# Hybrid layer with expert retrieval: the first group's four tiles by fetched rows, the second group's four dense, routing weights built all at once

## The chip, the cores and the metric

The kernel runs on one core of one Trainium2 chip. The metric is the device time of one execution in microseconds (us), as the median of several runs. The engines are TensorE (PE in the profile, its weight loads PEld), VectorE (DVE), ScalarE (ACT), GpSimd (POOL) and SyncE (SP). SyncE and GpSimd issue the DMAs of this kernel; the 16 DMA engines of the core carry them all.

## The reference: what is computed

One layer of a hybrid backbone over a prompt (128 tokens) and a sample (1024 tokens), model width 1024. A combined projection feeds a gMLP mixer (A) and a bidirectional gated recurrence, HGRN2 (B); both are merged, projected and added to the residual. Then comes the part that the change is about, the retrieval over 16384 single-neuron experts:

```
h  = rmsnorm(x) * (1 + scale2) + shift2
q  = (h @ w_q)  as 8 heads x 2 halves x 128
s  = q . sub_keys                       # 8 x 2 x 128 scores a token
v1, i1 = top16(s[:, :, 0]);  v2, i2 = top16(s[:, :, 1])
top 16 of the 256 sums v1 + v2  ->  idx = i1 * 128 + i2,  g = softmax(top 16)
a  = gelu(h . u_tab[idx]) * g           # 128 experts a token
x  = x + gate2 * sum(a * v_tab[idx])
```

At the end every token gets a last rmsnorm. Only the prompt's recurrent states and the normalised tokens are returned.

## The kernel before

**Tiles.** Tokens stand in nine tiles of 128: tile 0 is the prompt, tiles 1 to 8 the sample. Products of the sample are computed in two float32r parts a factor, as three matmuls (helper `mmx`, L126 to L131: high x high, low x high, high x low); `split` (L98 to L100) makes the parts, the high one on ScalarE, the low one on VectorE.

**Stages, in order.** The modulation vectors and the whole prompt (to about 340 us, without its retrieval); HGRN over the sample (340 to 705); the first group GA = [5, 6, 7, 8] (705 to 1116) and the second group GB = [1, 2, 3, 4] (1116 to 1700), both in `group`: gate and value projections (12 units of weights), merge (24 units), output projection (8), norm and transposes, queries with scores and top 16 (16 units). Then the dense pass, and the last norms.

**Two ways of retrieval.** For the tiles in `GATHER` = [0, 1, 2, 3] the experts are fetched row by row (`gather`): for each of 128 chosen experts, one indirect DMA on GpSimd brings a row of `u_tab` for each of 128 tokens (128 x 4 KB), one VectorE instruction multiplies it by the tokens and sums; then, per head, 16 rows of `v_tab` are fetched and added with their weights. That is 256 row instructions a tile. For the tiles in `DENSE` = [5, 6, 7, 8, 4] all 16384 experts are computed: for each of 128 expert tiles e, `hidden` multiplies the tokens (640 columns in two halves of 320) by `u`, gelu follows, the result is multiplied by the routing weights `Gt` and split, and multiplied by `v`. The sums of RES = 3 token tiles stay in PSUM (`out_res`), those of ROT = 2 more rotate: every GI = 4 expert tiles they are added to SBUF by VectorE (`out_rot`).

**Choosing and building.** `combine` picks the 16 best sums of each head of one token tile, on VectorE; it is a generator with about a dozen steps, and can be run for heads 0 to 3 and 4 to 7 separately. For a dense tile, `build_G` then writes the routing weights as a matrix experts x tokens: for every OT = 4 tokens one step compares an iota with the two indices (L516), weights one of the one-hots by the high and low half of g (L520 on ScalarE or L524 on VectorE, every second step, and L526), TensorE multiplies the pairs (L543), ScalarE evacuates (L546), and blocks of 32 tokens go to DRAM (`G_d`).

**Order.** Instructions are ordered by a scheduler at build time, with program order as priority. Filling work comes from three queues of generators (`choose_q`, `build_q`, `gather_q`). In the groups every unit of weights (`unit`, `tick`) advances them by `rate`; in the dense pass `fill` advances the fetched rows at each of its main VectorE instructions, and `paced` keeps a row's instruction behind an earlier instruction of the main stream. GA's choices and builds run beside GB; tile 4 is chosen and built behind GB (L988 to L990), beside two early expert tiles. Tiles 1 to 3 lie in DRAM (`tvi_d`) and are chosen inside the dense pass (`combine_late`). The tokens of the dense tiles pass through DRAM (`h2T_d`) into `h2D`. Fetched rows have NGR = 4 slots, and NGD = 2 more in the dense pass.

Of the kernel before, what the change touches and what calls it, by code (L numbers as in the profile page):

```python
# [28 lines left out]
RATE2 = (3, 4.5, 2)  # L29
RQ = 0.3  # L30
LATE = (3, 0.8)
LEAD = 60
AH = (1, 2)       # of how many blocks of one-hots ScalarE does the weighting
RATE = (4, 2.6, 0.5, 2.5, 6.1, 4.5)
# [17 lines left out]
def hybrid_kernel(ctx, tc, x_all, pos, c2t, w_ada, b_ada, wst, wspt, bsp, lbraw, vecs, fng, skt, state,  # L52
# [19 lines left out]
    h2T_d = dram.tile([2, 128, 8, TD], F32, name="h2T_d")  # L72
    o_d = dram.tile([NT, 128, 512], F32, name="o_d")
    tvi_d = dram.tile([NT, 128, 512], F32, name="tvi_d")
    h2r_d = dram.tile([NT, 128, D], F32, name="h2r_d")

# [5 lines left out]
    vec = consts.tile([128, 24], F32, name="vec")        # g1(8) g2(8) sgu(4) hgrn(4), channel on partition  # L82
# [6 lines left out]
    lb = consts.tile([128, 3, 8], F32, name="lb")        # lb, (1-lb)/2, (1+lb)/2  # L89

# [33 lines left out]
    def mmx(ps, a, b, first, last):  # L124
        """a.T @ b for operands in one float32 part or in two float32r parts"""
# [24 lines left out]
    # work that fills the engines beside the main stream: generators, advanced a step at a time  # L150
# [42 lines left out]
    # order of the six modulation vectors: shift1 scale1 gate1 shift2 scale2 gate2  # L193
# [74 lines left out]
    def proj_rows(u0, opd, n, evac, native, half=None):  # L268
        """token-major product with a 512 wide block (4 units); opd(k): parts [128, T]; evac(i, psum)"""
# [16 lines left out]
    def hgrn(pool, blocks, proj, vsrc, states):  # L286
        """blocks: (token tile, head) of each 128 columns; proj(j, evac): products for q, fw, bw"""
        NB = len(blocks)
        NTOK = NB * 128
        K2 = pool.tile([128, 2, NTOK], F32, name="K2")       # fw, bw  # L290
        Q2 = pool.tile([128, 2, NTOK], F32, name="Q2")       # bw, fw
        F2 = pool.tile([128, 2, NTOK], F32, name="F2")       # fw, bw
# [41 lines left out]
            # K: fw first halves by the total of the second, bw second halves by the total of the first  # L334
# [8 lines left out]
            # totals of the doubled segments: the second level in T2, the others in place of the gates  # L343
# [7 lines left out]
        T128 = tbase                                        # F2[:, d, T128 + block]  # L351
# [52 lines left out]
    C = {}  # L404
    GA, GB = [5, 6, 7, 8], [1, 2, 3, 4]
# [9 lines left out]
    def combine(gp, t, tv, ti, al=None, c4=None, V=V, h0=0, h1=8, res=None):  # L415
        """the 16 best sums of a head: products of the two lists, with (i+1)(j+1) <= 16"""
# [28 lines left out]
        if res is None:  # L445
            res = al("res", 384).rearrange("p (a b) -> p a b", a=3)    # i1, i2, g
# [3 lines left out]
        hk = lambda x: x[:, :, None, :].to_broadcast(SH)                     # over the list position  # L450
        lp = lambda x: x[:, :, :, None].to_broadcast(SH)                     # over the chosen
# [26 lines left out]
        # softmax over the 16 of a head  # L478
# [10 lines left out]
        if t in GATHER:  # L489
            ga = gat.tile([128, 128], F32, name=f"ga{t}")  # L490
            V.tensor_copy(ga, res[:, 2])
            ix = gat.tile([128, 128], I32, name=f"ix{t}")
            V.scalar_tensor_tensor(ix, res[:, 0], 128.0, res[:, 1], op0=OP.mult, op1=OP.add)
            gather_q.append(gather(t, ga, ix))
        else:
# [3 lines left out]
            rt = gp.tile([128, 2, 128], F16, name="rt", bufs=4)      # i2, i1  # L499
            V.tensor_copy(rt, pt[:, 0:256].rearrange("p (a b) -> p a b", a=2))  # L500
            rg = gp.tile([128, 128], F32, name="rg", bufs=4)         # g (scaled)
# [6 lines left out]
    def build_G(gp, i, rt, rg, gl, tags):  # L508
        SH = [128, 2, 128, OT]

        def one_hots(t0):
# [675 lines left out]
```

## Time and profile before

| | |
|---|---|
| time, median of 3 runs | 3696.43 us (3687.48 to 3701.36) |
| profiled execution, span | 3697.6 us |
| PE busy | 3351.2 us (91%) |
| DVE busy | 2840.2 us (77%) |
| ACT busy | 1157.4 us (31%) |
| POOL busy | 1440.8 us (39%) |
| DMA | 971.12 MB, mean 263 GB/s |
| fetched rows | 512 + 512 indirect DMAs of 512 KB |

The profile is one execution. Its span runs from the first to the last instruction; it lies 1.2 us above the median of the runs, and no time around it is added. A stretch (a row of the view by windows) gives the busy time of each engine with its number of instructions, then the clock that TensorE was granted as a share of the full one, the share of the DMA engines' time, and GB/s. A matmul's duration contains its pipeline, so TensorE's pace is read from the distance of starts.

### The profile page before, as it was taken

To read this page: it belongs to the slowest core of one execution; us is meant where nothing else is said; L and a number is where in the kernel's file an instruction comes from. 1 tells how busy PE (TensorE), PEld (TensorE's weight loads), DVE (VectorE), ACT (ScalarE), POOL (GpSimd) and SP (SyncE) were. 2 spreads that over 40 slices of the span, in tenths; PEclk is the share of its full clock that TensorE was granted. 3 is DMA by queue.
4 is the path that set the end of the run, shared out by engine and by line. 5 is a ranking of instruction groups with operands and counts; after the bars stand their busy time and mean duration, and the time that the engine had idled before them with its cause. 6 is when DMAs were issued, how large, how long until landed. Compare 5 with 4: busy or idle time off the path is not lost. (4 is left out here: it accounts for less than half of the span.)

```text
span 3697.6 us, 48818 instructions
## 1 busy us (share of the span) xinstructions
PE 3351.2 (91%) x17547; PEld 2757.2 (75%) x17547; DVE 2840.2 (77%) x5427; ACT 1157.4 (31%) x2075; POOL 1440.8 (39%) x1128
## 2 busy tenths in 40 slices
PE   7787889899797899888789999889999989999997
PEld 3265678777476676576688989788888878898996
DVE  1315698787499987588787889888888888888888
ACT  2511233432222387735322222222222222222222
POOL 0100632265311220000255554556555465655664
PEclk9899999999898999888799999999999999999998
DMA  7676854488842476441798898889988799989986
GB/s 267 226 272 208 297 189 153 158 292 307 296 161 97 163 278 252 172 165 75 257 327 307 316 335 286 311 298 330 326 308 316 256 327 338 318 301 328 328 313 249
DMA packets 361957, 971.12 MB, mean 263 GB/s; under 512 B 32721, under 2 KB 142673, under 8 KB 356081
## 3 DMA queue, kind: packets, MB, share of 16 engines
q0 software_dynamic: 149824, 546.37, 41.6%
q1 hardware_dynamic: 211888, 421.62, 33.1%
q8 instruction: 138, 2.26, 0.2%
q14 instruction: 107, 0.87, 0.1%
HBM read 897.07 MB, written 70.80 MB: 262 GB/s over the span
## 5 line engine op out<-in xcount | busy, mean ns | idle before, releaser
L795 POOL DMA_INDIRECT gu<-in_urow_dram,ix x512 | 693.5, 1354 | 1024.8 <-DVE jk L798 368.8
L808 POOL DMA_INDIRECT gv<-in_vrow_dram,ix x512 | 694.7, 1357 | 720.6 <-DVE acc L813 388.2
L798 DVE SCALAR_TENSOR_TENSOR jk<-gu,h2r 128x1024 f16<-128x1024 f32 x512 | 624.9, 1220 | 125.0 <-DMA gu<-in_urow_dram,ix 118.7
L813 DVE SCALAR_TENSOR_TENSOR acc<-gv,act,acc 128x1024 f32<-128x1024 f32 x508 | 651.3, 1282 | 65.9 <-DMA gv<-in_vrow_dram,ix 57.9
L129 PE MATMUL pH<-h2DH,uH 128*128 128x320 f32 x2016 | 626.1, 311 | 11.3 <-DVE accd L1045 10.4
L131 PE MATMUL pH<-h2DH,uL 128*128 128x320 f32 x2016 | 623.6, 310 | 3.4 <-DVE uL L100 3.4
L130 PE MATMUL pH<-h2DL,uH 128*128 128x320 f32 x2016 | 624.2, 310 | 0.0
L129 PEld LDWEIGHTS pH<-h2DH,uH 128*128 128x128 f32 x2016 | 380.5, 189 | 21.8 <-DVE accd L1045 15.6
L130 PEld LDWEIGHTS pH<-h2DL,uH 128*128 128x128 f32 x2016 | 380.3, 189 | 4.4
L131 PEld LDWEIGHTS pH<-h2DH,uL 128*128 128x128 f32 x2016 | 380.1, 189 | 4.3 <-DVE uL L100 4.3
L129 PE MATMUL pout<-vH,aH 128*128 128x512 f32 x768 | 298.5, 393 | 22.6 <-ACT vH L99 16.3
L99 ACT ACTIVATE vH<-vr 128x1024 fp32r<-128x1024 f32 x128 | 133.3, 1058 | 561.4 <-DMA vr<-in_vrow_dram 289.4
L130 PE MATMUL pout<-vL,aH 128*128 128x512 f32 x768 | 301.1, 392 | 6.2 <-DVE vL L100 6.2
L131 PE MATMUL pout<-vH,aL 128*128 128x512 f32 x768 | 300.4, 391 | 1.1 <-DVE aL L100 1.0
L129 PE MATMUL prot<-vH,aH 128*128 128x512 f32 x512 | 211.7, 414 | 57.8 <-DVE accd L1045 51.8
L99 ACT ACTIVATE wH<-wraw 128x1024 fp32r<-128x1024 f32 x118 | 125.1, 1060 | 439.4 <-PE pq L130 148.4
L100 DVE TENSOR_TENSOR vL<-vr,vH 128x1024 fp32r<-128x1024 f32 x128 | 156.0, 1220 | 93.7 <-ACT vH L99 93.6
L99 ACT ACTIVATE aH<-a 128x640 fp32r<-128x640 f32 x128 | 94.2, 736 | 368.5 <-DVE a L1062 363.7
L130 PE MATMUL prot<-vL,aH 128*128 128x512 f32 x512 | 208.0, 406 | 0.0
L131 PE MATMUL prot<-vH,aL 128*128 128x512 f32 x512 | 207.3, 405 | 0.0
L99 ACT ACTIVATE uH<-ur 128x1024 fp32r<-128x1024 f32 x126 | 133.4, 1058 | 234.1 <-PE pH L130 214.5
L543 PE MATMUL pG<-oh 128*128 128x128 f16 x1280 | 159.4, 281 | 35.0 <-ACT Gs L546 20.3
(343 smaller groups left out, 6407.7 us busy)
## 6 DMA issues: line engine op xcount, KB each, us to landing
wraw<-in_wst_dram SPq DMA_DIRECT2D x216, 512.0 KB, 4.4
vr<-in_vrow_dram SPq DMA_DIRECT2D x128, 512.0 KB, 6.4
ur<-in_ut_dram SPq DMA_DIRECT2D x126, 512.0 KB, 6.8
G_d<-Gs SPq DMA_DIRECT2D x40, 1024.0 KB, 4.1
Gt<-G_d SPq DMA_DIRECT2D x160, 256.0 KB, 8.7
wraw<-in_w_ada_dram SPq DMA_DIRECT2D x48, 512.0 KB, 4.4
gu<-in_urow_dram,ix POOLq DMA_INDIRECT x512, 6.3
gv<-in_vrow_dram,ix POOLq DMA_INDIRECT x512, 6.9
```

The lines of the kernel that those rows point to most:

```text
L99: A.activation(H, src, AF.Copy)
L100: return V.tensor_tensor(out=L, in0=src, in1=H.bitcast(F32), op=OP.subtract)
L129: P.matmul(ps, a[0], b[0], start=first, stop=False)
L130: P.matmul(ps, a[0], b[1], start=False, stop=False)
L131: P.matmul(ps, a[1], b[0], start=False, stop=last)
L543: P.matmul(pg[:, tt * 128:(tt + 1) * 128], oh[:, 0, :, tt], og[a][:, :, tt], start=(a == 0), stop=(a == 1))
L795: G.indirect_dma_start(out=ur, out_offset=None, in_=urow, in_offset=bass.IndirectOffsetOnAxis(ap=ix[:, c:c + 1], axis=0))
L798: paced(V.scalar_tensor_tensor(jk, ur, 1.0, h2r, op0=OP.mult, op1=OP.mult, accum_out=dots[:, k:k + 1]))
L808: G.indirect_dma_start(out=vr, out_offset=None, in_=vrow, in_offset=bass.IndirectOffsetOnAxis(ap=ix[:, c:c + 1], axis=0))
L813: paced(V.scalar_tensor_tensor(acc, vr, act[:, k:k + 1], acc, op0=OP.mult, op1=OP.add))
```

## The change

`GATHER` becomes [0, 1, 2, 3, 4] and `DENSE` [5, 6, 7, 8]; the groups swap tiles, so that GA = [1, 2, 3, 4] is the fetched group and GB the dense one. Tiles 1 to 4 are chosen beside GB, and their rows are fetched from there on, at the new rate of 3 a unit; `combine_late` and `tvi_d` are gone. The dense tiles' tokens stay in SBUF, `h2T_d` is gone. In the query loop of GB the choice of heads 0 to 3 of all four tiles is queued; the rest is run behind NE = 8 early expert tiles, and then the routing weights of all four tiles are built. A build step weights both halves in one VectorE instruction, and ScalarE takes no part in it. The dense pass has 512 columns in one product, one rotating tile, and fetches as many rows a step as are left. Row slots: six, two in the dense pass, four more from its ninth expert tile on. The product of a fetched row is written in place.

```diff
-NGR = 4           # slots of fetched rows, and those that the dense pass adds
+NGR = 6
-AH = (1, 2)       # of how many blocks of one-hots ScalarE does the weighting
-RATE = (4, 2.6, 0.5, 2.5, 6.1, 4.5)
+NE = 8
+RATE = (4, 2.6, 3, 1.5, 0, 4.5)
-GATHER = [0, 1, 2, 3]                             # token tiles whose experts are fetched row by row
-DENSE = [5, 6, 7, 8, 4]                           # token tiles that meet every expert
+GATHER = [0, 1, 2, 3, 4]
+DENSE = [5, 6, 7, 8]
...
-    GA, GB = [5, 6, 7, 8], [1, 2, 3, 4]
+    NRES = [1]
+    GA, GB = [1, 2, 3, 4], DENSE
...
-            if t0 // OT % AH[1] < AH[0]:
-                for tt in range(OT):
-                    A.activation(og[:, tt, :], oh[:, 1, :, tt], AF.Copy, scale=rg[:, t0 + tt:t0 + tt + 1])
...
-            V.tensor_tensor(out=ol, in0=oh[:, 1], in1=gl[:, 1:2, t0:t0 + OT].to_broadcast(SH[:1] + SH[2:]),
-                            op=OP.mult)
+            V.tensor_tensor(out=ow, in0=oh[:, 1:2].to_broadcast(SH),
+                            in1=gl[:, :, None, t0:t0 + OT].to_broadcast(SH), op=OP.mult)
...
-            onf = gp.tile([128, 512], F32, name="on", bufs=2)
+            onf = gp.tile([128, 512], F32, name="on", bufs=1)
...
-        if tiles is GB:
-            rate.update(choose=RATE2[0], build=RATE2[1], gather=RATE2[2])
...
+                  for z, p, tag in (("H", C["ep"], "m8"), ("L", gp, "g8"))] if tiles is GA else bigpair("h2D", TD)
...
-            if tiles is GB and t in GATHER:
-                # looked at in the dense pass
-                for z, x in enumerate((tv[i], ti[i].bitcast(F32))):
-                    nc.sync.dma_start(tvi_d[t][:, z * 256:(z + 1) * 256], x.rearrange("p a b c -> p (a b c)"))
-                late.append(t)
-            elif i in halves:
+            if i in halves:
...
-                jk = gat.tile([128, D], F16, name="jk", bufs=1)
-                paced(V.scalar_tensor_tensor(jk, ur, 1.0, h2r, op0=OP.mult, op1=OP.mult,
+                paced(V.scalar_tensor_tensor(ur, ur, 1.0, h2r, op0=OP.mult, op1=OP.mult,
...
     def hidden(a, u):
-        for hs in range(2):
-            ph = ptp("pH")
-            projT(ph[:, :HS], u, lambda k: cut(h2D, slice(None), k, slice(hs * HS, (hs + 1) * HS)))
-            A.activation(a[:, hs * HS:(hs + 1) * HS], ph[:, :HS], AF.Gelu_apprx_tanh)
+        ph = ptp("pH")
+        projT(ph, u, lambda k: cut(h2D, slice(None), k))
+        A.activation(a, ph, AF.Gelu_apprx_tanh)
...
-    advance(gather_q, 10000)
-    for e in range(2):
+    for e in range(NE):
+        if e % 4 == 0:
+            a4 = C["ep"].tile([128, 4, 512], F32, name="a4", tag="m8", bufs=2)
         u = unit(0, src=ut[e])
-        early.append(gat.tile([128, D], F32, name="a0", tag=("h2r", "acc")[e], bufs=1)[:, 0:TD])
+        early.append(a4[:, e % 4])
         hidden(early[e], u)
     advance(choose_q, 1000)
     advance(build_q, 1000)
...
+    left = 256 * len(GATHER) - nrow[0]
+    rows_of[:] = [(gat, NGR)] * NGR + [(dp, NGD)] * NGD
...
-        advance(gather_q, RATE[4] * GI / (3 * GI + 2 * ROT))
+        advance(gather_q, 1.02 * left / 128 * GI / (3 * GI + 2 * ROT))
...
+            if e == NE:
+                epx.close()
+                ex = ctx.enter_context(tc.tile_pool(name="ex", bufs=1, side="left", reuse_waits="tile"))
+                rows_of.extend([(ex, 4)] * 4)
```

## Rows read from the trace of the kernel before

**Rows 1.** Stretches: busy per engine (instructions), granted clock, DMA share, GB/s.
```profile
705.00:1116.00 411.00, 368.09 (x1523) 271.91 (x1523) 307.63 (x787) 108.14 (x172) 163.54 (x138) 0.95 0.75 257
919.00:1005.00 86.00, 67.35 (x168) 31.95 (x167) 40.55 (x47) 14.08 (x27) 30.66 (x36) 0.89 0.91 314
1116.00:1220.00 104.00, 84.95 (x354) 66.55 (x353) 98.20 (x398) 33.25 (x48) 14.58 (x13) 0.90 0.30 99
1116.00:1700.00 584.00, 524.05 (x2595) 381.04 (x2594) 485.87 (x1528) 319.05 (x679) 74.21 (x69) 0.94 0.50 181
1719.00:1769.00 50.00, 33.43 (x256) 28.42 (x256) 39.31 (x85) 47.26 (x128) 0.00 (x0) 0.51 0.31 127
1782.00:3660.00 1878.00, 1789.64 (x9825) 1613.25 (x9826) 1567.38 (x2120) 460.45 (x671) 1056.71 (x772) 0.98 0.89 313
```

**Rows 2.** Timeline of PE in the dense pass: start, duration, engine, operation.
```profile
2518.44 0.31 PE L131 MATMUL pH<-h2DH,uL 128*128 128x320 f32 x1
2518.59 0.31 PE L129 MATMUL pH<-h2DH,uH 128*128 128x320 f32 x1
...
2524.12 0.39 PE L130 MATMUL pout<-vL,aH 128*128 128x512 f32 x1
2524.35 0.39 PE L131 MATMUL pout<-vH,aL 128*128 128x512 f32 x1
```

**Rows 3.** Groups by line and form, 1782 to 3660: count, busy us, mean ns.
```profile
L795 POOL DMA_INDIRECT gu<-in_urow_dram,ix x384 | 527.3, 1373 | 653.5 <-DVE jk L798 241.9 <-DMA Gt<-G_d 223.3 <-DVE acc L813 81.7
...
L813 DVE SCALAR_TENSOR_TENSOR acc<-gv,act,acc 128x1024 f32<-128x1024 f32 x380 | 487.5, 1283 | 27.0 <-DMA gv<-in_vrow_dram,ix 19.7
L798 DVE SCALAR_TENSOR_TENSOR jk<-gu,h2r 128x1024 f16<-128x1024 f32 x384 | 468.7, 1221 | 85.0 <-DMA gu<-in_urow_dram,ix 79.7
...
L100 DVE TENSOR_TENSOR vL<-vr,vH 128x1024 fp32r<-128x1024 f32 x128 | 156.0, 1220 | 93.7 <-ACT vH L99 93.6
L100 DVE TENSOR_TENSOR uL<-ur,uH 128x1024 fp32r<-128x1024 f32 x126 | 153.6, 1220 | 22.1 <-ACT uH L99 21.5 <-DMA vr<-in_vrow_dram 0.5
...
L100 DVE TENSOR_TENSOR aL<-a,aH 128x640 fp32r<-128x640 f32 x128 | 105.2, 822 | 64.7 <-ACT aH L99 64.7
L1062 DVE TENSOR_TENSOR a<-a,Gt 128x640 f32<-128x640 f32 x127 | 103.9, 818 | 5.6 <-ACT a L981 5.6
...
L1045 DVE TENSOR_TENSOR accd<-accd,prot 128x512 f32<-128x512 f32 x120 | 81.6, 680 | 5.3 <-PE prot L131 5.3
```

**Rows 4.** Groups of VectorE by line, 1116 to 1700: the build steps.
```profile
L516 DVE TENSOR_TENSOR oh<-iota,rt 128x1024 f16<-128x1024 f16 x128 | 87.5, 688 | 60.5 <-PE pG L543 55.8 <-ACT Gs L546 2.2 <-ACT oh L520 1.9
...
L526 DVE TENSOR_TENSOR oh<-oh,gl 128x512 f16<-128x512 f16 x128 | 50.6, 418 | 0.2
...
L524 DVE TENSOR_TENSOR oh<-oh,gl 128x512 f16<-128x512 f16 x64 | 26.8, 418 | 0.2
```

**Rows 5.** Timelines of PE and DVE behind the last query: first hidden product, last choice.
```profile
1699.68 0.39 PE L129 MATMUL pH<-h2DH,wH 128*128 128x320 f32 x1
...
1704.38 0.27 DVE L430 TENSOR_TENSOR cand<-tv 128x32 f32<-128x32 f32 x2
...
1710.13 1.23 DVE L463 TENSOR_TENSOR prod<-cmp,di 128x1024 f16<-128x1024 f16 x1
...
1718.09 0.22 DVE L458 TENSOR_TENSOR res<-prod 128x64 f32<-128x64 f16 x1
```

**Rows 6.** Timeline of DVE: first and last build instruction, first dense multiplication.
```profile
1719.55 0.68 DVE L516 TENSOR_TENSOR oh<-iota,rt 128x1024 f16<-128x1024 f16 x1
...
1765.22 0.42 DVE L526 TENSOR_TENSOR oh<-oh,gl 128x512 f16<-128x512 f16 x1
...
1780.93 1.56 DVE L1062 TENSOR_TENSOR a<-a,Gt 128x640 f32<-128x640 f32 x2 [14.82 <-DMA Gt<-G_d]
```

**Rows 7.** Stretches of the dense pass with most DMA traffic, columns as above.
```profile
2340.00:2400.00 60.00, 59.65 (x337) 54.10 (x336) 51.89 (x66) 14.75 (x22) 38.93 (x30) 0.99 0.98 359
3030.00:3060.00 30.00, 28.46 (x144) 24.11 (x144) 25.60 (x24) 5.96 (x8) 15.57 (x12) 1.00 1.04 390
```

More of the change, by code (lines that the diff above doesn't have):

```diff
@@ L445, in combine @@
         if res is None:
-            res = al("res", 384).rearrange("p (a b) -> p a b", a=3)
+            res = gp.tile([128, 384], F32, name="res4", bufs=NRES[0]).rearrange("p (a b) -> p a b", a=3)
         r3 = lambda x: x[:, hs].rearrange("p (a b) -> p a b", a=nh)
@@ L489, in combine @@
         if t in GATHER:
-            ga = gat.tile([128, 128], F32, name=f"ga{t}")
+            ga = gat.tile([128, 128], F32, name="ga", bufs=5)
             V.tensor_copy(ga, res[:, 2])
-            ix = gat.tile([128, 128], I32, name=f"ix{t}")
+            ix = gat.tile([128, 128], I32, name="ix", bufs=5)
             V.scalar_tensor_tensor(ix, res[:, 0], 128.0, res[:, 1], op0=OP.mult, op1=OP.add)
@@ L500, in combine @@
             V.tensor_copy(rt, pt[:, 0:256].rearrange("p (a b) -> p a b", a=2))
-            rg = gp.tile([128, 128], F32, name="rg", bufs=4)
+            rg = gp.tile([128, 128], F32, name="rg", bufs=1)
             V.tensor_scalar(rg, pt[:, 256:384], 16384.0, None, op0=OP.mult)
@@ L640, in group @@
         else:
-            mg0 = [gp.tile([128, 4, 512], F32, name="mg", tag="m8", bufs=2) for _ in range(2)]
+            mg0 = [C["ep"].tile([128, 4, 512], F32, name="mg", tag="m8", bufs=2) for _ in range(2)]
             mg = lambda k: mg0[k // 4][:, k % 4, :]
@@ L670, in group @@
             s = slice(half * 512, half * 512 + 512)
-            gt1 = gp.tile([128, 512], F32, name="gate1", tag="on", bufs=2)
+            gt1 = gp.tile([128, 512], F32, name="gate1", tag="on", bufs=1)
             nc.sync.dma_start(gt1, gate_d[cnd:cnd + 1, s].to_broadcast([128, 512]))
@@ L687, in group @@
             advance(build_q, 10000)
-            h2 = [[gp.tile([128, 4, 512], F32R, name="h2" + z, tag=tag, bufs=2) for _ in range(2)]
-                  for z, tag in (("H", "m8"), ("L", "g8"))]
+            h2 = [[p.tile([128, 4, 512], F32R, name="h2" + z, tag=tag, bufs=2) for _ in range(2)]
+                  for z, p, tag in (("H", C["ep"], "m8"), ("L", gp, "g8"))] if tiles is GA else bigpair("h2D", TD)
             class Two:
@@ L698, in __getitem__ @@
                     return self.a[k // 4][p, k % 4, t]
-            h2 = [Two(a) for a in h2]
+            if tiles is GA:
+                h2 = [Two(a) for a in h2]
         gl = [i for i in range(n) if tiles[i] in GATHER]
@@ L711, in group @@
         norm_T(gp, xn, 1, cnd, h2, back if gl else None)
-        for i in range(n):
-            if tiles[i] in DENSE:
-                c0 = DENSE.index(tiles[i]) * 128
-                for z in range(2):
-                    for kh in range(2):
-                        nc.sync.dma_start(h2T_d[z][:, kh * 4:kh * 4 + 4, c0:c0 + 128],
-                                          h2[z].a[kh][:, :, i * 128:(i + 1) * 128].bitcast(F32))
         tv = [gp.tile([128, 8, 2, 16], F32, name="tv", bufs=n) for _ in range(n)]
@@ L730, in group @@
                 for i in split_at:
-                    res = gp.tile([128, 384], F32, name="res", bufs=1).rearrange("p (a b) -> p a b", a=3)
+                    res = gp.tile([128, 384], F32, name="res4", bufs=NRES[0]).rearrange("p (a b) -> p a b", a=3)
                     halves[i] = res
@@ L758, in group @@
                 choose_q.append(combine(gp, t, tv[i], ti[i]))
-    def combine_late(t):
-        cols = []
-        def al(name, n, dt=F32):
-            w = n if dt in (F32, U32) else (n + 1) // 2
-            if not cols or cols[-1][1] + w > 1024:
-                cols.append([dp.tile([128, 1024], F32, name="late", tag="grow", bufs=NGD), 0])
-            c = cols[-1]
-            c[1] += w
-            x = c[0][:, c[1] - w:c[1]]
-            return x if dt == F32 else x.bitcast(dt)
-        q = lambda x: x.rearrange("p (a b c) -> p a b c", a=8, b=2)
-        tvi = al("tvi", 512)
-        nc.sync.dma_start(tvi, tvi_d[t])
-        yield from combine(None, t, q(tvi[:, 0:256]), q(tvi[:, 256:512].bitcast(U32)), al,
-                           lambda name: row(name).bitcast(F16), Paced())
-    rows_of, rowc, late, nrow = [], [0], [], [0]
+        return h2
+    rows_of, rowc, nrow = [], [0], [0]
     def row(name):
@@ L881, in consts_of @@
             nc.sync.dma_start(r["bsb"], bsp[None].to_broadcast([128, 4, 128]))
-            sm33 = gp.tile([128, 1024], F32, name="sm33", tag="sm", bufs=1) if not iota else gp.tile(
+            sm33 = gp.tile([128, 1024], F32, name="sm33", tag="sm", bufs=1) if not iota else C["ep"].tile(
                 [128, 4, 512], F32, name="sm33", tag="m8", bufs=2).rearrange("p a b -> p (a b)")
@@ L961, in hybrid_kernel @@
     CF.update(h512=6)
+    NRES[0] = 4
+    epx = ExitStack()
+    C["ep"] = epx.enter_context(tc.tile_pool(name="ep", bufs=1, side="left", reuse_waits="tile"))
     gp = phg.enter_context(tc.tile_pool(name="gp", bufs=1, side="right", reuse_waits="tile"))
@@ L998, in hybrid_kernel @@
     vt = vrow.rearrange("(e p) d -> e p d", p=128)
-    late_q = deque(combine_late(t) for t in late)
-    C["coff"], C["clen"], C["cj"] = load_cs3(dp, row("cs32"))
-    nrow[0] = 0
-    lates = len(late_q)
+    left = 256 * len(GATHER) - nrow[0]
+    rows_of[:] = [(gat, NGR)] * NGR + [(dp, NGD)] * NGD
     def fill(ins):
         anchor(ins, KEEP)
-        k = lates - len(late_q)
-        if late_q and nrow[0] >= 256 * k - LEAD:
-            owed[0] = owed.get(0, 0) + LATE[k > 0]
-            while owed[0] >= 1 and lates - len(late_q) == k:
-                owed[0] -= 1
-                if next(late_q[0], 0) == 0:
-                    late_q.popleft()
-        busy = late_q and nrow[0] >= 256 * (lates - len(late_q)) - LEAD
-        rows_of[:] = [(gat, NGR)] * NGR + [(dp, NGD)] * (0 if busy else NGD)
-        advance(gather_q, RATE[4] * GI / (3 * GI + 2 * ROT))
+        advance(gather_q, 1.02 * left / 128 * GI / (3 * GI + 2 * ROT))
     def load_split(src, nm, bufs):
```

33 lines of the change are left out of this document (9 added, 24 removed).

## The prediction, made before the changed kernel was run

> **What bounds the kernel now.** I read the stretches first, one per stage. Three stages matter. While the second group runs (1116 to 1700 us), VectorE is busy 486 of 584 us and TensorE 524 [rows 1]. Between the last query product and the dense pass everything waits for one choice of experts and one build of routing weights. The dense pass (1782 to 3660) takes more than half of the span: 1878 us with TensorE busy 1790, VectorE 1567 and DMA at 313 GB/s [rows 1]. What TensorE's busy time is worth is read from the distance of neighbouring starts: 0.147 us for a product with 320 columns, 0.227 us for one with 512 [rows 2]. One expert tile needs 48 of the first kind (16 x 3) and on average 30 of the second ((3 + 2) x 2 x 3). Over the pass that is 126 x 48 x 0.147 = 889 and 128 x 30 x 0.227 = 872, or 1761 of 1878 us: TensorE bounds the dense pass, with 6% of stalls.
>
> VectorE is second. Durations by name [rows 3]: 768 row instructions (1.221 and 1.283, mean 1.252) 962; expert products times weights 104; splits 105 + 154 + 156; the rotating sum about 84; three late choices about 83 (6 halves of 13.9, below); two last norms about 10. That is 1658, while the stretch has 1567 busy, because neighbours overlap. So I count VectorE as durations times 0.945.
>
> **The change, part by part.** Two tiles are exchanged in role. Fetched tiles are now 0 to 4 (five), dense ones 5 to 8 (four), and the fetched tiles 1 to 4 make up the first group.
>
> *Rows that are fetched early.* Each weight unit advances the fetch by its rate. HGRN: 20 units x 4 = 80. First group: 44 x 2.6 + 16 x 0.78 = 127, both as before. Second group: 44 x 3 + 16 x 0.9 = 146 against the 49 that tile 0 still needed. So 353 are done ahead of the dense pass and 1280 - 353 = 927 are left for it, against 768.
>
> *First group.* The back transposes of fetched tokens move here from the second group (four tiles for three), and one slot instead of two for the gate's operands makes each of four tiles wait for a load; the stores of dense tokens go. I take +5 us (-10 to +20); two more row slots speak for the lower end.
>
> *Second group.* VectorE decides. Of its 486 us, the weight building of four tiles goes: 128 steps x (0.688 + 0.418 + half of 0.418) = 168 [rows 4], times 0.945 = 159. Take off also 49 rows (58) and a last norm (5), and 264 is left: main stream, the four choices of the first group, and the first quarter or so of the next. Added are 146 rows: 146 x 1.252 x 0.945 = 173, and the norm: 442 in all. Some 50 of it falls into the output-and-norm stage, which took 86 us in the first group, where VectorE has slack [rows 1]; the other 392 run at the 0.944 share that VectorE reached where it was the bound (98.2 of 104 us) [rows 1]: 415. With 6 us for the single gate slot: 415 + 86 + 6 = 507, so -77. Bounds: 411, what the first group takes with little choosing beside it, and 584, this stage now [rows 1].
>
> *Behind the last query.* Before: first hidden product at 1699.7, first dense multiplication at 1780.9, so 81 us [rows 5, 6]. In it half a choice of one tile takes 13.9 us on VectorE [rows 5], then 32 build steps from 1719.5 to 1765.2, 1.43 us each [rows 6], paced by ScalarE (47.3 of 50 us busy [rows 1]). From the last step to the first multiplication lie 16 us (evacuation, store, load). After: the first-half choices of four tiles have 32 steps, of which 8 units x 1.5 = 12 fall into the query loop; 20 remain, 20/8 x 13.9 = 35 us, and four second halves are 56. Then four builds follow: 128 steps. ScalarE loses its weighting, and VectorE does one comparison and one multiplication of 1024 halves each. The comparison is 0.688 [rows 4]; the multiplication isn't in the trace and lies between 0.688 (same layout) and 1.23 (a 1024 product whose innermost step is broadcast [rows 5]); its innermost four are contiguous in both inputs, so I take 0.688. That is 1.30 us a step at 0.945, 166 us. Sum on VectorE: 5 (last top 16) + 7 (six splits of the early expert tiles) + 91 + 4 (copies of indices and weights) + 166 = 273, plus the same 16: 289. So +208 us. No rows are fetched in this time and TensorE has 8 early expert tiles (8 x 24 x 0.227 = 44 us) and short weight products to do; nothing hides the rest. Bounds: 1.05 us a step, TensorE's pace for its products (33.4 us for 32 steps, with half of the full clock granted in that stretch, 1.2 of 2.4 GHz [rows 1]), -32; 1.23 for the multiplication, +66; choices that start only behind the sixth early tile, +27.
>
> *Dense pass.* TensorE: (120 x 24 + 128 x 24) x 0.227 = 1351 us; it is no longer the bound. VectorE: 927 x 1.252 = 1161; products and their splits at 512 columns 128 x 2 x 0.68 = 174 (0.68 is the 512-column sum [rows 3]); weight splits 128 x 1.22 + 120 x 1.22 = 303; the sum of one rotating tile 44; last norms 20; total 1702, times 0.945 = 1608. GpSimd: 927 x 1.373 = 1273 busy [rows 3]. DMA: now 313 GB/s x 1878 us = 588 MB. After: 159 more fetches of 524 kB (+83), six expert loads less (-3), a fifth of the routing weights less (-8): about 660 MB. Stretches of before carry 359 GB/s for 60 us and 390 for 30 us with TensorE busy for 0.95 of it or more [rows 7]. I take 365, near the longer one since the stage lasts 30 times as long: 1808 us, -70. This is above all three engines, so DMA and the in-order row instructions on VectorE set the pass.
>
> *End.* One dense tile less in the last norms: -3 of 38 us.
>
> Sum against the profiled execution (span 3697.6): 3697.6 + 5 - 77 + 208 - 70 - 3 = 3760.6. The span lies 1.2 us above the median of the runs, so 3759.
>
> **The rivals.** *DMA stays at its ceiling lower than I take it.* If the 359 GB/s of the best 60 us is what lasts, the pass takes 660/0.359 = 1838 us, and if that ceiling is used as well as TensorE's is now (1761/1878 = 0.94), 1960; the middle, 1900, gives 3851. For it: every fetched row stands in VectorE's queue ahead of the splits, so late rows stop the stream. Against it: 30 us at 390, and twelve row slots instead of six once the eighth expert tile has passed. The Trainium skill (DMA: Bandwidth & Descriptors, Specifications) gives about 358 GB/s as the share of HBM of one core; the 60 us agree with it and the 30 us at 390 do not. By that figure alone the pass would be 1844 us and the whole 3795 (an estimate from the page).
>
> *Faster: the dense pass is left to VectorE alone.* Now TensorE's 1761 become 1351, and if DMA follows, 1608 at the 0.944 share is 1703 us: -175 instead of -70, total 3654. It needs 388 GB/s, the best 30 us, all through. The change breaks even where the pass takes 1745 us, at 378 GB/s.
>
> *Building costs more.* The multiplication at 1.23 adds 66 us and choices behind the early splits 27: 3825 to 3852. For it: such a 1024 product exists; against it, its layout.
>
> **How the numbers follow.** Chances: forecast, 3700 to 3810, 0.50; DMA ceiling 0.24; costly building 0.11; faster 0.15. The likeliest gives 3759. The range: a tenth lies below 3650 (VectorE-bound pass) and a tenth above 3880 (ceiling and building together). A measurement here tells apart about 0.5%, 18 us. Faster by more: 0.13; within: 0.11 (the rest of the faster case and the low end of the forecast, where group two nears its 411 us); slower: 0.76.
>
> **What would show it.** Right: a second group of about 507 us with VectorE over 0.9 in its first 36 units; some 290 us from the first hidden product to the first dense multiplication, VectorE busy nearly throughout, DMA nearly idle and half of the full clock granted; a dense pass with TensorE busy well below 0.9, DMA near 365 GB/s, and row instructions that wait for their DMA. Wrong: a dense pass under 1745 us, build steps of about 1.6 us or more, weight steps already done beside the early tiles, or a second group still at 584.

## The result and the profile after

The changed kernel takes 3776.05 us (median of four runs, 3774.59 to 3782.57) against 3698.89 us for the kernel before on the same chip: a ratio of 1.0224, 95% interval 1.0202 to 1.0246. It is slower by 2.2%. The profiled execution has a span of 3774.9 us, 77.3 us more than the 3697.6 of before, so the stages of the two spans can be set side by side. Each stage is cut at the same events in every kernel of this study: the last product of the HGRN stage, the first row product of the second group, the first hidden product behind the last query, the first and the last dense multiplication by routing weights. By this cut HGRN of the kernel before ends at 721.3 us, where the sections above say 705.

| stage, us | before | after | difference | forecast |
|---|---|---|---|---|
| up to the end of HGRN | 721.3 | 697.9 | -23.4 | 0 |
| first group | 395.6 | 388.0 | -7.6 | +5 |
| second group | 582.8 | 509.8 | -73.0 | -77 |
| behind the last query | 81.2 | 268.3 | +187.1 | +208 |
| dense pass | 1875.2 | 1869.4 | -5.8 | -70 |
| end | 41.5 | 41.5 | 0.0 | -3 |
| sum | 3697.6 | 3774.9 | +77.3 | +63 |

These are the stretches of the kernel after, with the columns of [rows 1]: the first group; the second group and its first two parts; the time behind the last query in three parts, then as a whole; the dense pass; the end.

```profile
697.90:1085.90 388.00, 357.31 (x1493) 264.89 (x1492) 301.38 (x774) 110.49 (x171) 158.48 (x133) 0.96 0.72 258
1086.00:1596.00 510.00, 417.37 (x1530) 281.74 (x1529) 450.56 (x1387) 109.87 (x161) 217.97 (x168) 0.93 0.65 230
1086.00:1203.00 117.00, 86.78 (x344) 65.24 (x343) 107.92 (x322) 30.11 (x45) 56.29 (x43) 0.88 0.65 221
1203.00:1381.00 178.00, 150.18 (x497) 97.03 (x496) 168.34 (x370) 31.27 (x42) 105.66 (x72) 0.93 0.79 280
1596.00:1640.00 44.00, 44.00 (x189) 35.12 (x189) 43.92 (x223) 19.97 (x23) 0.00 (x0) 1.00 0.18 61
1640.00:1681.00 41.00, 3.66 (x14) 2.01 (x12) 41.00 (x241) 5.47 (x8) 0.00 (x0) 0.56 0.00 1
1681.00:1851.00 170.00, 131.18 (x1017) 113.14 (x1018) 168.94 (x284) 128.71 (x252) 4.60 (x4) 0.50 0.49 198
1596.00:1864.00 268.00, 180.21 (x1228) 151.37 (x1227) 253.86 (x744) 156.12 (x287) 4.60 (x4) 0.59 0.38 149
1864.00:3733.00 1869.00, 1508.34 (x5894) 1174.14 (x5895) 1570.72 (x1977) 403.63 (x531) 1244.65 (x922) 0.90 0.95 348
3733.00:3775.00 42.00, 13.36 (x59) 10.71 (x58) 34.09 (x34) 6.76 (x12) 6.12 (x11) 0.72 0.55 218
```

In the second group VectorE is the third figure: 107.92 of 117 us and 168.34 of 178, shares of 0.92 and 0.95, as it was where it set the pace before. Behind the last query VectorE is hardly idle up to 1851 us (43.92 of 44, 41.00 of 41, 168.94 of 170), while the fetching engine GpSimd shows 0, 0 and 4.6 us. DMA is half idle there: a share of 0.18, 0.00 and 0.49 in the three parts, 0.38 in the whole. In the dense pass TensorE has fallen from 0.95 to 0.81 of the time, VectorE stays at 0.84, and what is nearly full is DMA: a share of 0.95 where [rows 1] has 0.89. (The share adds up the times of packets, so it has no hard end at 1: [rows 7] has 1.04.)

The groups of VectorE and ScalarE while the weights are built (1681 to 1851; count, busy us, mean ns, idle before) answer [rows 4]:

```profile
L511 DVE TENSOR_TENSOR oh<-iota,rt 128x1024 f16<-128x1024 f16 x128 | 88.0, 688 | 0.6
L513 DVE TENSOR_TENSOR oh<-oh,gl 128x1024 f16<-128x1024 f16 x128 | 82.4, 684 | 0.0
L533 ACT ACTIVATE Gs<-pG 128x256 f32<-128x256 f32 x252 | 128.7, 660 | 42.2 <-PE pG L530 34.7 <-ACT Gs L533 7.3
```

The multiplication whose price the trace of before did not show takes 0.684 us, the price of its layout, not 1.23. One step is 170/128 = 1.33 us by the stretch and 1.30 was forecast. ScalarE now only evacuates. The end of the stage, from VectorE's timeline, is a wait for stored weights to come back, as in [rows 6]:

```profile
1849.57 1.29 DVE L513 TENSOR_TENSOR oh<-oh,gl 128x1024 f16<-128x1024 f16 x2
1864.04 1.90 DVE L1008 TENSOR_TENSOR a<-a,Gt 128x512 f32<-128x512 f32 x3 [13.18 <-DMA Gt<-G_d]
```

The costliest groups of rows in the whole profile after (they answer the first rows of [rows 3], which are of the dense pass alone) show prices that hardly moved; the counts did, from 512 to 640 of each kind:

```profile
L752 POOL DMA_INDIRECT gu<-in_urow_dram,ix x640 | 858.7, 1342 | 1018.6 <-DVE gu L754 397.4
L764 POOL DMA_INDIRECT gv<-in_vrow_dram,ix x640 | 876.3, 1369 | 644.8 <-DVE acc L769 276.4
L769 DVE SCALAR_TENSOR_TENSOR acc<-gv,act,acc 128x1024 f32<-128x1024 f32 x635 | 813.4, 1281 | 9.4 <-DMA gv<-in_vrow_dram,ix 7.3
L754 DVE SCALAR_TENSOR_TENSOR gu<-gu,h2r 128x1024 f32<-128x1024 f32 x640 | 765.7, 1218 | 54.3 <-DMA gu<-in_urow_dram,ix 53.5
```

In the dense pass alone (1864 to 3733) the row instructions on VectorE wait less for their rows than before: 24 us, where the same two kinds of [rows 3] have 79.7 and 19.7.

```profile
L769 DVE SCALAR_TENSOR_TENSOR acc<-gv,act,acc 128x1024 f32<-128x1024 f32 x450 | 576.8, 1282 | 0.2
L754 DVE SCALAR_TENSOR_TENSOR gu<-gu,h2r 128x1024 f32<-128x1024 f32 x461 | 550.6, 1218 | 24.1 <-DMA gu<-in_urow_dram,ix 23.9
```

Who waits for DMA instead is seen at ScalarE, which makes the first copy of each loaded expert tile. Its waits (us in total, times, longest), first in the kernel before, then in the kernel after:

```profile
ACT vH L99 <- DMA vr<-in_vrow_dram: 289.4, 68, 9.0
ACT uH L99 <- DMA ur<-in_ut_dram: 16.6, 6, 6.0
```

```profile
ACT vH L94 <- DMA vr<-in_vrow_dram: 763.6, 119, 22.2
ACT uH L94 <- DMA ur<-in_ut_dram: 222.0, 74, 11.8
```

ScalarE waits 306 us for the expert loads before and 986 after, and the longest wait has grown from 9 to 22 us. That the loads are late because they share the 16 DMA engines with the fetched rows is a reading. The wait alone does not show it, since ScalarE has idle time to spend (404 of 1869 us busy): the first experiment below still has 681 us of it, at a DMA share of 0.74. The experiments decide.

### The profile page after: what moved, and what is told of

It is laid out like the page before. It is cut to its first block, busy times and chain, and to the rows that moved or that the text cites. A ratio compares the mean times of both kernels' runs of the same rounds, so it can differ in the third digit from the quotient of the medians.

```text
span 3774.9 us, 40448 instructions
## 1 busy us (share of the span) xinstructions
PE 3089.8 (82%) x13456; PEld 2327.5 (62%) x13456; DVE 3010.8 (80%) x5716; ACT 1000.7 (27%) x1576; POOL 1780.6 (47%) x1382
## 5 line engine op out<-in xcount | busy, mean ns | idle before, releaser
L752 POOL DMA_INDIRECT gu<-in_urow_dram,ix x640 | 858.7, 1342 | 1018.6 <-DVE gu L754 397.4
L764 POOL DMA_INDIRECT gv<-in_vrow_dram,ix x640 | 876.3, 1369 | 644.8 <-DVE acc L769 276.4
L769 DVE SCALAR_TENSOR_TENSOR acc<-gv,act,acc 128x1024 f32<-128x1024 f32 x635 | 813.4, 1281 | 9.4 <-DMA gv<-in_vrow_dram,ix 7.3
L754 DVE SCALAR_TENSOR_TENSOR gu<-gu,h2r 128x1024 f32<-128x1024 f32 x640 | 765.7, 1218 | 54.3 <-DMA gu<-in_urow_dram,ix 53.5
L124 PE MATMUL pH<-h2DH,uH 128*128 128x512 f32 x960 | 402.4, 419 | 65.5 <-DVE accd L987 39.2
L126 PE MATMUL pH<-h2DH,uL 128*128 128x512 f32 x960 | 399.3, 416 | 52.6 <-DVE uL L95 52.6
L125 PE MATMUL pH<-h2DL,uH 128*128 128x512 f32 x960 | 396.7, 413 | 0.0
L124 PEld LDWEIGHTS pH<-h2DH,uH 128*128 128x128 f32 x960 | 192.5, 201 | 125.1 <-DVE accd L987 49.9
L126 PEld LDWEIGHTS pH<-h2DH,uL 128*128 128x128 f32 x960 | 191.6, 200 | 112.9 <-DVE uL L95 66.7
L125 PEld LDWEIGHTS pH<-h2DL,uH 128*128 128x128 f32 x960 | 191.8, 200 | 45.3
```

What stands on the lines that cost most here:

```text
L124: P.matmul(ps, a[0], b[0], start=first, stop=False)
L125: P.matmul(ps, a[0], b[1], start=False, stop=False)
L126: P.matmul(ps, a[1], b[0], start=False, stop=last)
L752: G.indirect_dma_start(out=ur, out_offset=None, in_=urow, in_offset=bass.IndirectOffsetOnAxis(ap=ix[:, c:c + 1], axis=0))
L754: paced(V.scalar_tensor_tensor(ur, ur, 1.0, h2r, op0=OP.mult, op1=OP.mult, accum_out=dots[:, k:k + 1]))
L764: G.indirect_dma_start(out=vr, out_offset=None, in_=vrow, in_offset=bass.IndirectOffsetOnAxis(ap=ix[:, c:c + 1], axis=0))
```

## The experiments

The theory to begin with: the dense pass of the changed kernel is set by the bytes that DMA carries, so the time TensorE saves there is not to be had, and the 268 us behind the last query, in which DMA is half idle and no rows are fetched, are what the change pays. The first rival: the row instructions in VectorE's queue set the pass, and DMA is merely busy. The second: the number of slots in which fetched rows land sets it. A third stands in the expectations: TensorE at its lower granted clock (0.90 in the pass, 0.98 before).

A time without a number of runs is that of a single run. Executions of one kernel lay up to 27 us apart (3700 to 3727 in ten runs), so a smaller difference between single runs settles nothing.

**Bytes or VectorE.** Two kernels take away one of them each.

*Every second fetch is left out, VectorE's instructions stay* (the same edit stands at the second kind of row):

```diff
-                ur = row("gu")
                 c = h * 16 + k
-                G.indirect_dma_start(out=ur, out_offset=None, in_=urow,
-                                     in_offset=bass.IndirectOffsetOnAxis(ap=ix[:, c:c + 1], axis=0))
+                if k % 2 == 0:
+                    ur = row("gu")
+                    G.indirect_dma_start(out=ur, out_offset=None, in_=urow,
+                                         in_offset=bass.IndirectOffsetOnAxis(ap=ix[:, c:c + 1], axis=0))
```

> The changed kernel with every second row fetch left out: the VectorE instruction of an odd row works on the row before it, so VectorE's work is the same and the fetched bytes are half (the retrieval of the fetched tiles is not computed). In the dense pass about 243 of 651 MB go. Theory A (DMA traffic sets the dense pass): the pass falls from 1872 us to what VectorE allows, 1574 busy at a share of 0.92 to 0.95, 1660 to 1710. Theory B (VectorE's in-order queue sets it, with DMA waits only beside it): 1830 to 1870. Theory C (TensorE with its lower granted clock sets it): unchanged within 20 us.

*Every row is fetched, VectorE works on half of its columns* (both row instructions):

```diff
-                paced(V.scalar_tensor_tensor(ur, ur, 1.0, h2r, op0=OP.mult, op1=OP.mult,
+                paced(V.scalar_tensor_tensor(ur[:, 0:512], ur[:, 0:512], 1.0, h2r[:, 0:512], op0=OP.mult, op1=OP.mult,
```

> The changed kernel with all rows fetched, but VectorE multiplies and adds only 512 of the 1024 columns of a row (half of the retrieval of the fetched tiles is not computed). VectorE loses about 927 x 0.55 = 510 us of its 1574 busy in the dense pass; bytes are the same. Theory A: the dense pass stays at 1800 to 1870 us, because 651 MB still have to come in, at 348 to 365 GB/s. Theory B: it falls in the proportion of VectorE's work, to 1400 to 1500 us. Theory C: unchanged. The second group, where VectorE decides, becomes shorter by some 50 to 80 us under all three.

Measured: 3566.64 and 3673.8 us. The dense stretch of the first, then the dense stretch and the end of the second:

```profile
1853.60:3520.20 1666.60, 1461.53 (x5901) 1144.04 (x5902) 1563.71 (x1977) 404.53 (x531) 645.69 (x461) 0.94 0.74 248
```

```profile
1805.30:3553.00 1747.70, 1477.20 (x5896) 1160.95 (x5897) 1065.68 (x1876) 399.78 (x529) 931.85 (x854) 0.91 0.94 352
3553.00:3672.00 119.00, 12.97 (x58) 10.40 (x56) 76.09 (x134) 6.70 (x13) 76.13 (x80) 0.57 0.94 372
```

Without half of the row bytes and with the same VectorE work (1563.71 against 1570.72 us) the pass falls by 203 us, to 1667, and there VectorE is busy for 0.94 of it: the next bound, at which it stops. TensorE's work is the same, so the third rival, which expected no change, fell. With a third less VectorE work (1065.68) and all the bytes, DMA stays at 0.94 and 352 GB/s. The pass looks shorter by 122 us, but rows were left over and ran in the end, which has grown from 41.5 to 119: pass and end together take 1866.7 instead of 1910.9 us, -44. So the pass alone lies under the 1800 us that the theory asked for at the least, and only pass and end together agree with it. The bytes of both are the same: 352 GB/s x 1747.7 + 372 x 119 = 659 MB here, 348 x 1869.4 + 218 x 42 = 660 MB in the kernel after. VectorE's work in pass and end is 463 us less (1141.8 against 1604.8) and that is worth 44 us; the bytes of the pass are 238 MB less without half of the fetches (248 x 1666.6 = 413 against 651), and that is worth 203. The bytes set the pass. Two limits of this: leaving out fetches takes away GpSimd's instructions along with the bytes, and no run gave the pass more slots than it has. The second group, forecast to fall by 50 to 80 us with half of the columns, fell by 42 (509.8 to 467.4), with 77 us less of VectorE's work.

**Slots.** The changed kernel with four slots instead of six, once as it is and once also with the product of the row in a tile of its own, as before:

```diff
-NGR = 6
+NGR = 4
```

> The changed kernel with four instead of six slots for fetched rows (so as before the change; the dense pass still adds two and four). The stages up to the end of the first group took 1086 us after the change and 1116 before, where I had forecast 5 us more. If the two slots are the cause, the end of the first group moves back to 1105 to 1125 us; if it is the row's product in place or the exchange of tiles, it stays at 1080 to 1095. The dense pass, with 10 slots instead of 12, changes by less than 20 us if traffic sets it, and grows by 30 us or more if it lacks rows in flight.

```diff
-                paced(V.scalar_tensor_tensor(ur, ur, 1.0, h2r, op0=OP.mult, op1=OP.mult,
+                jk = gat.tile([128, D], F16, name="jk", bufs=1)
+                paced(V.scalar_tensor_tensor(jk, ur, 1.0, h2r, op0=OP.mult, op1=OP.mult,
```

> The changed kernel with four row slots, as in the run with four slots, but with the product of a fetched row written to a half-precision tile of its own, as before the change, instead of in place. With four slots and the product in place the first group ended at 1145 us, 28 us later than before the change with four slots, and the whole took 3919 us. If the product in place is what four slots don't bear (the slot is written by VectorE and comes free later), the first group ends at 1110 to 1125 and the whole falls by 60 us or more, to 3860 or less. If the exchange of the groups costs it, both stay within 10 and 20 us.

Measured: 3919.34 and 3965.12 us, 143 and 189 more than with six. The second group and the dense stretch with four slots in place, then the dense stretch with four slots apart:

```profile
1144.60:1685.80 541.20, 427.30 (x1529) 288.19 (x1528) 452.11 (x1387) 110.02 (x161) 213.69 (x168) 0.90 0.63 217
1954.40:3875.70 1921.30, 1527.97 (x5902) 1188.87 (x5903) 1574.02 (x1978) 403.67 (x531) 1226.49 (x923) 0.89 0.93 339
```

```profile
1935.20:3918.50 1983.30, 1501.52 (x5899) 1167.93 (x5900) 1573.98 (x1975) 403.67 (x531) 1223.61 (x921) 0.87 0.91 328
```

Slots are the second thing that counts. With four, DMA's share falls from 0.95 to 0.93 and 0.91 and the pass takes 52 and 114 us more, at the same VectorE work. The stages ahead of it lose too. The second group takes 541.2 us for 509.8, with the same work on VectorE. It begins at 1144.6 and 1132.2 us, with six slots at 1085.9, and in the kernel before at 1116.9, or 1125.6 with the product in place (below). So at four slots the product in place costs HGRN and the first group 9 to 12 us, the rest of the change 15 (both kernels apart) to 19 (both in place), and the two more slots give back 59 (both in place).

Neither expectation was met in full: with four slots the first group was to end at 1105 to 1125 us, and ended 20 us later; with the product apart the whole was to fall by 60 us or to stay within 20, and rose by 46.

**Rows beside the building.** If the dense pass pays for bytes and the 268 us before it have DMA half idle, rows moved there should be cheaper than in the pass:

```diff
-    advance(choose_q, 1000)
-    advance(build_q, 1000)
+    while choose_q or build_q:
+        advance(choose_q if choose_q else build_q, 1)
+        advance(gather_q, 1)
```

> The changed kernel, complete, with one fetched row issued at each step of the choices and builds behind the last query (some 190 rows), which the dense pass then has not to fetch. A row costs VectorE about 1.17 us in the build stretch, where VectorE is busy all the time, so that stretch grows from 268 to 440 to 490 us. Theory A: each row is worth 524 kB / 348 GB/s = 1.5 us in the dense pass, which falls by 250 to 290 us: in all 40 to 70 us faster than the changed kernel, 3705 to 3735. Theory B: a row is worth as much in both places: within 15 us of 3776. Theory C: slower by the 170 to 220 us that the build stretch grows.

Measured: 3727.82 us (four runs), 1.0082 of before (1.0051 to 1.0114). By the medians that is 36 us above the kernel before, measured beside it at 3692.12, where the changed kernel lay 77 above. The stage of the building grew to 500 us, more than the 440 to 490 expected. The time behind the last query and the dense pass:

```profile
1599.80:2100.30 500.50, 190.10 (x1231) 144.72 (x1229) 473.81 (x1035) 161.24 (x294) 265.07 (x195) 0.55 0.79 283
2100.30:3707.50 1607.20, 1434.96 (x5904) 1145.94 (x5905) 1355.18 (x1694) 400.06 (x522) 1041.58 (x732) 0.94 0.94 345
```

GpSimd's instructions fall from 922 to 732 in the pass, 190 fetches gone: 262 us less there, 1.38 us for each. In the building they cost 232 us, 1.22 each, which is VectorE's price of a row instruction [rows 3]. So a row costs a VectorE instruction in the one place and its share of DMA in the other, and moving it gains the difference. (This profiled execution is the longest of the four, 15 us above their median.)

**The building on two engines.** That the stage of the building is VectorE's is tested by giving every second step's weighting of the high half to ScalarE, as the kernel before did with some of it, on top of the last edit (`rg`, which ScalarE now reads, gets four buffers, `ga` and `ix` four instead of five):

```diff
+            if t0 // OT % 2 < 1:
+                og = o4[:, 2].rearrange("p (t j) -> p t j", t=OT)
+                for tt in range(OT):
+                    A.activation(og[:, tt, :], oh[:, 1, :, tt], AF.Copy, scale=rg[:, t0 + tt:t0 + tt + 1])
...
-            V.tensor_tensor(out=ow, in0=oh[:, 1:2].to_broadcast(SH),
```

> The changed kernel with a fetched row at each choice and build step behind the last query, and in every second build step the high half of the weights weighted on ScalarE, with the changed kernel's own early rates. Against the run with the rows alone (behind 500 us, dense 1607, whole 3728): 64 steps lose 512 columns of VectorE, 64 x 0.27 = 17 us to 64 x 0.42 = 27 us, so behind 475 to 485 and the whole 3700 to 3712. If ScalarE (evacuations and weighting together) sets those steps instead, behind stays at 495 to 510. To beat the kernel before (3693) the dense pass would have to fall too, which nothing in this edit does.

Measured: 3709.59 us (ten runs), 1.0045 of before (1.0027 to 1.0063).

```profile
1596.20:2081.90 485.70, 194.72 (x1231) 147.60 (x1229) 458.67 (x1036) 237.43 (x550) 251.03 (x195) 0.55 0.81 292
2081.90:3671.60 1589.70, 1427.30 (x5905) 1137.47 (x5906) 1355.44 (x1693) 399.98 (x522) 1031.12 (x732) 0.95 0.95 348
```

VectorE has 15 us less, and the stage is 15 us shorter: 485.7, just above the 475 to 485 expected. By itself that is not clear of the differences between executions, since the dense pass, which the edit does not touch, differs by 17.5 us too; VectorE's share of the stage, 0.95 and 0.94, says the same. It is the best complete kernel tried in place of the change and 0.45% slower than the kernel before. Its dense pass is at the same 348 GB/s.

The same with more rows fetched early (rates of 5 and 3 instead of 4 and 2.6 in HGRN and the first group):

> The changed kernel with rows fetched beside choices and builds (3728 us), and on top: every second build step weights its high half on ScalarE, as before the change, and 40 more rows are fetched in HGRN and the first group (rates 5 and 3). If VectorE sets the build stretch, it loses 0.27 us in every second of 128 steps, some 17 to 28 us with what ScalarE adds, to 470 to 485; 40 rows fewer in the dense pass are 55 to 60 us at its traffic, of which the earlier stages take back 20 to 30: 3675 to 3700 in all. If those stages take back all of it, 3700 to 3715.

Measured: 3722.39 us (four runs), 1.0073 of before (1.0049 to 1.0098), above both ranges expected. HGRN ended at 721.1 instead of 694.8 us and the first group took 398.0 instead of 388.4, while the dense pass fell only to 1579, by 11: there the rows cost more than in the pass. That it is because their instructions on VectorE stand beside work that needs it is not shown.

**The place of the rows in VectorE's queue.** In the changed kernel a row instruction stands no earlier than behind the main stream's instruction two back; here four back:

```diff
-KEEP = 2
+KEEP = 4
```

> The changed kernel with the row instructions allowed behind the main stream's instruction four back instead of two back (KEEP 4); work, bytes and slots unchanged. If the dense pass of 1870 us is set by what DMA can carry (348 GB/s at a share of 0.95), the order cannot give much: 1850 to 1890, whole 3755 to 3795. If the order of the queue still costs it, as the in-place runs of the kernel before suggest, the pass falls below 1830 or rises above 1910.

Measured: 3789.14 us. The dense pass:

```profile
1870.70:3746.90 1876.20, 1519.61 (x5905) 1178.87 (x5906) 1568.40 (x1971) 404.68 (x531) 1231.55 (x919) 0.90 0.95 346
```

It takes 7 us more than without the edit, less than executions differ by. So earlier row instructions gain nothing in a pass that DMA sets.

**The product in place, in the kernel before.** The change also writes the row product into the fetched row's own tile. That part alone, done to the kernel before:

```diff
-                jk = gat.tile([128, D], F16, name="jk", bufs=1)
-                paced(V.scalar_tensor_tensor(jk, ur, 1.0, h2r, op0=OP.mult, op1=OP.mult,
+                paced(V.scalar_tensor_tensor(ur, ur, 1.0, h2r, op0=OP.mult, op1=OP.mult,
```

> The kernel before the change with one part of it alone: the product of a fetched row is written in place. If that costs with four slots, the first group ends some 20 to 30 us later than 1117 us and the dense pass, with six slots, grows too: 3730 to 3800 in all. If not, the time stays within 15 us of 3692.

Measured: 3850.02 us, 156 more than before and above the range expected, and 139 of it in the dense pass (2014.6). Its VectorE work is that of before (1557 us, and 1565 before by the same cut), and it waits for rows. The dense pass, and VectorE's group there:

```profile
1792.10:3806.70 2014.60, 1828.61 (x9807) 1633.23 (x9808) 1557.44 (x2117) 457.30 (x670) 1068.49 (x772) 0.95 0.84 291
L797 DVE SCALAR_TENSOR_TENSOR gu<-gu,h2r 128x1024 f32<-128x1024 f32 x384 | 461.3, 1221 | 252.8 <-DMA gu<-in_urow_dram,ix 252.3
```

In [rows 3] the same wait is 79.7 us. Three more kernels looked for the cause. With five slots (and fewer buffers for four other tiles, to make room):

> The kernel before the change with five row slots instead of four (seven in the dense pass), paid for by the product in place, one slot for the gate's operands and two for the chosen indices and weights. If slots are what made the stages up to the first group 31 us shorter after the change with six, five should give 10 to 25 us there and up to 20 in the dense pass: 3650 to 3680. If the product in place takes it back, or the single gate slot does, the time stays within 10 us of 3692 or rises.

Measured: 3769.6 us (five runs), 1.0209 of before (1.0184 to 1.0234), where 3650 to 3680 was hoped for. With the slot and the smaller buffers it is 80 us less than in place with four, 47 of them in the dense pass (1967.9), which does not make up for the loss. But the first group ends at 1090.5 us, 26 earlier than before: a slot gives time there without any exchange of tiles. With the product in place but written as half words, as the separate tile has it:

```diff
-                paced(V.scalar_tensor_tensor(ur, ur, 1.0, h2r, op0=OP.mult, op1=OP.mult,
+                paced(V.scalar_tensor_tensor(ur[:].bitcast(F16)[:, :D], ur, 1.0, h2r, op0=OP.mult, op1=OP.mult,
```

> The kernel before with the row product written in place, into the first half of the fetched row's own tile, as half words: the bytes that VectorE writes are those of the kernel before, and the instruction order of every engine is the same as in the run that wrote whole words in place (3850 us against 3694). Theory that the order of the instructions made that loss: 3840 to 3860 again. Rival, that the doubled bytes written by VectorE disturb the arriving rows: 3690 to 3720.

Measured: 3853.74 us, with the wait for rows at 245.1 us: the bytes written are not the cause. By the traces the two runs in place have the same order of instructions on every engine.

With whole words in place and KEEP 4:

> The kernel before with the row product in place (3850 us), and the row instructions now allowed to stand behind the main stream's instruction four back instead of two back in VectorE's queue (KEEP 4). Nothing else is changed: same slots, same bytes, same work. Theory that the order decides: the dense pass moves by 30 us or more from its 2015, most likely down to 1900 to 1970, whole 3740 to 3810. Rival, that something else in writing in place costs the time whatever the order: within 20 us of 3850.

Measured: 3825.53 us, dense pass 1993.7, 21 less. That is under the 30 us that the theory of the order asked for, so it is not borne out; the whole is 24 us less, just beyond the 20 that the rival allowed, and single runs do not part them. And in the changed kernel, at four slots, the product in place was faster (1921) than apart (1983). What the separate tile gives to the kernel before stays open: the instruction orders of the kernels with and without it differ on every engine, which fits an effect of the order, but no run isolates it.

## Why the prediction was right, and where it was not

The forecast of 3759 us was 17 us low (14 by the spans), inside its main case (3700 to 3810), and its direction held. By the stages, the second group came out within 4 us, and it was in part luck that the whole came so near, since errors of -57 and +71 us nearly cancelled: -36 us (HGRN and first group), +4 (second group), -21 (behind the last query), +64 (dense pass), +3 (end), together +14.

**Second group: right.** Forecast 507 us, measured 509.8. VectorE's sum was 442 us and the stretch has 450.56; its first two parts run at the share that was taken from [rows 1]. What the working had no term for is the slots: with four of them the same work (452.11 us) took 541.2.

**Behind the last query: right in its cause, 21 us too high.** The building was put at 166 us and took 170, with one comparison and one multiplication of 0.69 us each, VectorE busy throughout and TensorE at half of the full clock: granted 0.50, the 1.2 GHz level, behind a stretch in which it had worked 3.66 of 41 us. Of the tail, 14 us from the last multiplication to the first dense one, 16 were forecast. The excess was in the choices: with the first splits 107 us were counted, and 85 are there (1596 to 1681). One reason is the price: half a choice was put at 13.9 us, and where one follows the other here the last ones begin 12 us apart. They began beside the early expert tiles at once (43.92 of 44 us), so the rival by which they would start only behind the sixth tile fell, and so did the one with the multiplication at 1.23. Of the signs named for this time, a DMA nearly idle came only in part: its share is 0.38.

**Dense pass: the bound was named rightly, its speed was not.** The step that failed is "I take 365". The bytes were 348 x 1869.4 = 651 MB against 660 forecast; at 365 GB/s that is 1783 us. The 365 was interpolated between stretches of [rows 7], in which the DMA share is 0.98 and 1.04. At a share of 0.95 the stretch of 359 GB/s would carry 359/0.98 x 0.95 = 348, what the whole pass then showed, and the runs with rows moved (345 and 348) and with VectorE relieved (352) too. The view had the share in the column beside the rate, and so a warning that a rate at a share of 1 need not last. But the 0.95 stands in no row of before, and the rate per share is no constant either (248/0.74 = 335 with half of the fetches, 372/0.94 = 396 at the end of the run with half the columns): the 348 could not have been read off beforehand. The prediction let the in-order row instructions on VectorE set the pass together with DMA, and named row instructions that wait for their rows as a sign; they wait 24 us in the pass, less than before, and with half of their columns pass and end lost only 44. On this term the rival of a lower ceiling was the better forecast: 1838 us from the 359 GB/s, and 1869 came; near its upper end, 1960, the pass came only with four slots (1921 and 1983). The Trainium skill (DMA: Bandwidth & Descriptors, Specifications) gives about 358 GB/s as one core's share of HBM; 348 sustained lies 3% under it, and the last 119 us of the run with half the columns lie over it, at 372. An estimate from the page's figure and the forecast bytes was 1844.

The rival by which the pass is left to VectorE was put at 1703 us. It is real behind the other: with half of the fetches the pass took 1667 with VectorE at 0.94. It would have needed 388 GB/s, which no long stretch reached.

**HGRN and first group: the mis-sized term.** +5 was forecast (-10 to +20) and -31 came. The two more slots had been put at "the lower end"; the runs with four slots give them 59 us, against 28 that the rest of the change costs, the product in place included. In HGRN, which has the same fetch rate in both kernels, no difference had been expected at all, and 23 came. Without the slots the change would have cost some 220 us instead of 77 (3919 against 3699), and 266 with the product apart (3965).

**End: no difference** where -3 was expected.

The prediction also named what would show it wrong: weight steps beside the early tiles did not occur, the choices did run beside them, and no pass fell under 1745 us in a kernel that does all the work without moving rows out of the pass.

## What to carry to other kernels

Time saved on the bounding engine is worth only what the next resource leaves, and for DMA that is a rate that a long stage can hold (341 to 352 GB/s here), not that of the best 30 or 60 us. Work gathered behind a last dependency should bring along something for the engines that lie idle: here one fetched row at each step of choosing and building took back some 40 of the 77 us, since its price changes from a DMA transfer to a VectorE instruction. Change a buffer count and an exchange of roles in separate steps: the two slots were worth 143 us, more than the whole net loss, and hid part of what the exchange costs.

## What the runs showed of the hardware that was not expected

- DMA held a share of 0.94 to 0.95 and 341 to 352 GB/s in every dense pass of the changed kernel with six slots and all rows, over 1579 to 1876 us, however VectorE's queue was ordered or relieved. With four slots it was 0.91 to 0.93 and 328 to 339.
- Writing a row's product in place instead of into a tile of its own, with VectorE's busy time unchanged (1557 against 1565 us), cost the kernel before 156 us, and in the changed kernel with four slots it gained 46. The bytes written play no part (3850 and 3854 us). These are single runs, and the cause is open.
